# A decoder step on one core: 1,768 products of constants, lying in all 92 activation slots, ahead of the first conditioning product

## The chip, the cores and the metric

The kernel runs on one core of one Trainium2 chip. The metric is the device time of one execution in microseconds (us). Engines are called by the profile's names: PE is TensorE's matmul, PEld its weight load, DVE is VectorE, ACT is ScalarE, POOL is GpSimd, and SP issues the transfers.

## The reference, cut to what matters

One layer for 288 tokens (256 of a prompt, 8 times 4 of samples) with 2048 features:

```
mod = (silu(c) @ w_ada + b_ada)                  # conditioning, 9 vectors
h = rms(x) * (1 + sc_m) + sh_m
proj = h @ w_in                                  # gates, conv, u, v
merged = sigmoid(ga) * (ya @ w_pa) + sigmoid(gb) * (yb @ w_pb)
x = x + gt_m * (merged @ w_out)
h2 = rms(x) * (1 + sc_f) + sh_f
gate, up = split(h2 @ w_ffn_in)
x = x + gt_f * ((silu(gate) * up) @ w_ffn_out)
y = rms(x) * g_final
```

All data are float32. The kernel computes all of this before and after the change.

## The kernel before, in words

Activations lie with features on the 128 partitions and the 288 tokens along the row, one tile of 128 features after the other. A product is taken with both factors split in a high and a low part of type fp32r: `triple` (L222) issues three matmuls, high times high (L224), high times low (L227), low times high (L229), so that of each weight tile's two parts the high one is loaded into the array twice in a row. The moving operand is an activation of 288 columns (298 in the first products, where 10 conditioning columns ride along). It lies in one of 92 equal "slots" of SBUF (`SLOTS`, `slot`, L112), handed out and taken back by a pool. Weights stream in as 1 MB blocks into seven buffers (`RAW`, tag `raw`). ACT makes the high parts of a block (L448) and DVE the low ones (L454, or L243 in the paced first part).

The order of PE's work is the order in which the code is written. It starts with fillers, `warm` (L568), which multiply a constant bf16 tile `wb` by itself into a bank called `idle` that nobody reads: 24 of them, while the first transfers land. Then come the first conditioning product (`Ada.run`, L388, units `a0`) with fillers in between, and `first_tile` (L690): DVE turns the conditioning sums (L402), scales (L676, L678), ACT makes the high part of the first activation tile (L677), and PE begins with the weights `w0` (L501). `second_tile` (L701) does the same with unit `a1` for the second activation tile, whose weights are `wK`. The square sums, the normalisation and the later conditioning units are woven into the blocks that follow.

SP issues the loads in a fixed order in the head: `a0` (two buffers), `w0`, piece 0 of `x`, `a1` (two buffers), piece 1 of `x`, `wK`, then `wA` and the other pieces of `x` in turns. A load into a `raw` buffer waits until the last reader of what lay there is done, and what stands behind it on SP waits too.

Of the kernel before, what the change touches and what calls it, by code (L numbers as in the profile page):

```python
# [8 lines left out]
F32 = mybir.dt.float32  # L9
F32R = mybir.dt.float32r  # L10
# [4 lines left out]
P = 128  # L15
D = 2048
T = 288
TP = 256
TU = T + 10
# [4 lines left out]
SLOTS = 92  # L24
RAW = 7
# [59 lines left out]
def decoder_kernel(tc, d):  # L85
    nc = tc.nc
    from contextlib import ExitStack

    with ExitStack() as es:
        def pool(name, bufs=1, **kw):  # L90
            return es.enter_context(tc.tile_pool(name=name, bufs=bufs, **kw))

        pc = pool("const")
        pw = pool("wstream")
        pslot = pool("slots", SLOTS)
        ptmp = pool("tmp", 5)
        pps = pool("psum", 4, space=bass.MemoryType.PSUM)
        with tc.manual_schedule(engines={nc.tensor.engine}):
            _body(tc, nc, d, pc, pw, pslot, ptmp, pps)


def _body(tc, nc, d, pc, pw, pslot, ptmp, pps):
    ids = [0]

    def nm(s):
        ids[0] += 1
        return f"{s}_{ids[0]}"

    def const(name, shape, dt=F32):
        return pc.tile(shape, dt, tag=name, name=name)  # L110

    def slot(dt=F32, shape=(P, T)):  # L112
        return pslot.tile(list(shape), dt, tag="s", name=nm("s"), padded_shape=[P, TU])
# [4 lines left out]
    def psmain():  # L118
        return pps.tile([P, 512], F32, tag="main", name=nm("pm"), bufs=4)
# [4 lines left out]
    V, A, G, PE, SY = nc.vector, nc.scalar, nc.gpsimd, nc.tensor, nc.sync  # L124
# [227 lines left out]
    class Step:  # L352
        defer = False
        raw = None
# [209 lines left out]
    wb = const("wb", [P, 288], BF16)  # L564
    G.memset(wb, 1.0)
    idle = psmain()
# [475 lines left out]
        tail.close()  # L1042


    rh1 = h1.__getitem__
    def at(main, plan):
        out, n = [], 0
        for s in main:
            out.append(s)
            if isinstance(s, Blk):  # L1050
                n += 1
                out += plan.pop(n, [])
        assert not plan
        return out
# [70 lines left out]
    n = len(steps)  # L1125
# [30 lines left out]
    for s in steps:  # L1156
# [11 lines left out]
        i = pos[id(s)]  # L1168
# [124 lines left out]
```

## Time and profile before

| | |
|---|---|
| median of 2 runs | 1624.98 us (1624.95 to 1625.01) |
| the profiled execution | 1625.02 us, of which the span from the first to the last instruction is 1623.2 |
| mean granted PE clock | 0.998 |
| matmul records on PE | 12,645, some 11,300 of them of the split products |
| DVE, ACT, POOL busy | 63%, 45%, 1% of the span |
| HBM read | 352.46 MB, 219 GB/s over the span |

The page gives the share of the span in which each engine is busy, and the chain of work that ended last. A matmul's record (its "mean ns") lasts longer than the distance to the next one's start, since matmuls are pipelined. What one costs is the distance between starts, and over a stretch without a gap that is the stretch divided by the number of matmuls in it.

### The profile page before, as it was taken

How to read it: one execution, taken by the hardware profiler on the slowest of the kernel's cores; microseconds unless marked ns; L12 is line 12 of the kernel's file. 1: busy time of each engine (PE TensorE's matmuls, PEld its weight loads, DVE VectorE, ACT ScalarE, POOL GpSimd, SP SyncE). 2: the span in 40 equal slices, each digit the busy share in tenths (PEclk: the TensorE clock that was granted, in tenths of full speed). 3: DMA queues.
4: the chain of work that ended last, by engine and by line, in shares of the span. 5: the costliest groups of instructions: out<-in, count | busy, mean ns of one | idle time of the engine just before them, and what ended most of it. 6: DMA issues, size and time to landing. Idle time of an engine off the chain costs nothing.

```text
span 1623.2 us, 31599 instructions
## 1 busy us (share of the span) xinstructions
PE 1613.2 (99%) x12645; PEld 1549.3 (95%) x12645; DVE 1015.8 (63%) x2196; ACT 736.2 (45%) x1358; POOL 21.8 (1%) x66
## 2 busy tenths in 40 slices
PE   9999999999999999999999999999999999999997
PEld 8998999999999999999999999999999999999997
DVE  6676788877755567667744555555555555555565
ACT  5533344643444334456633444444444444444454
POOL 0000000000000000011000000000000000000000
PEclk9999999999999999999999999999999999999999
DMA  9887866777877666654576556453464434645341
GB/s 376 324 318 286 313 238 212 273 284 289 298 292 309 261 260 228 241 178 158 185 307 263 207 180 209 156 173 110 164 229 157 168 121 161 225 157 172 110 161 59
DMA packets 59140, 357.60 MB, mean 220 GB/s; under 512 B 6736, under 2 KB 9840, under 8 KB 28272
## 3 DMA queue, kind: packets, MB, share of 16 engines
q1 hardware_dynamic: 58704, 355.45, 60.0%
q8 instruction: 99, 1.62, 0.4%
q14 instruction: 49, 0.40, 0.1%
q10 hardware_dynamic: 288, 0.13, 0.0%
HBM read 352.46 MB, written 3.09 MB: 219 GB/s over the span
## 4 chain that ended last, share of the span: by engine, by line
PE 98%; DMA 1%; DVE 0%; DVEq 0%; ACT 0%; issue 0%; ACTq 0%
PE pm L224 31%; PE pm L227 31%; PE pm L229 30%; PE ada L388 5%; DMA raw<-in_wK 1%; DMA raw<-in_w 0%; DVE st L1023 0%; DMA ct<-in_c 0%; PE px L227 0%; PE px L818 0%; PE px L224 0%; PE px L229 0%; PE px L859 0%; PE px L198 0%; PE px L860 0%; PE px L861 0%
## 5 line engine op out<-in xcount | busy, mean ns | idle before, releaser
L224 PE MATMUL pm<-s,hi 128*128 128x288 f32 (+1 forms) x3750 | 1108.9, 296 | 0.0
L227 PE MATMUL pm<-s,hi 128*128 128x288 f32 (+1 forms) x3750 | 1105.0, 295 | 0.0
L229 PE MATMUL pm<-s,lo 128*128 128x288 f32 (+1 forms) x3738 | 1101.3, 295 | 0.0
L448 ACT CAST hi<-raw 128x512 fp32r<-128x512 f32 (+1 forms) x963 | 587.4, 612 | 812.0 <-PE pm L227 776.7
L454 DVE TENSOR_TENSOR lo<-raw,hi 128x512 fp32r<-128x512 f32 (+1 forms) x849 | 577.2, 681 | 439.2 <-ACT hi L448 426.8
L224 PEld LDWEIGHTS pm<-s,hi 128*128 128x128 f32 x3750 | 705.1, 188 | 15.2 <-issue 13.3
L227 PEld LDWEIGHTS pm<-s,hi 128*128 128x128 f32 x3750 | 704.7, 188 | 0.0
L229 PEld LDWEIGHTS pm<-s,lo 128*128 128x128 f32 x3738 | 702.7, 188 | 0.0
L243 DVE TENSOR_TENSOR lo<-raw,hi 128x512 fp32r<-128x512 f32 x111 | 74.7, 676 | 29.6 <-ACT hi L448 28.9
L388 PE MATMUL ada<-raw,cs 128*32 128x512 f32 (+2 forms) x1152 | 88.3, 452 | 0.0
L388 PEld LDWEIGHTS ada<-raw,cs 128*32 128x32 f32 x1152 | 30.9, 110 | 44.7 <-issue 42.0
L766 DVE TENSOR_TENSOR s<-pm,s 128x288 f32<-128x288 f32 x72 | 32.9, 457 | 19.8 <-PE pm L229 19.8
L298 DVE TENSOR_TENSOR s<-t,s 128x288 fp32r<-128x288 f32 (+1 forms) x76 | 34.6, 459 | 6.4 <-ACT s L296 6.4
L296 ACT CAST s<-t 128x288 fp32r<-128x288 f32 (+1 forms) x76 | 32.5, 433 | 12.9 <-DVE t L798 12.4
L338 DVE SCALAR_TENSOR_TENSOR x<-pm,mod,x 128x256 f32<-128x256 f32 x79 | 37.5, 475 | 0.0
L944 DVE SCALAR_TENSOR_TENSOR t<-t,pm 128x288 f32<-128x288 f32 x42 | 19.1, 454 | 20.6 <-PE pm L229 20.6
L758 DVE TENSOR_TENSOR s<-pm,s 128x288 f32<-128x288 f32 x48 | 21.8, 454 | 10.4 <-PE pm L229 9.5
L337 DVE TENSOR_TENSOR t<-pm,mod 128x32 f32<-128x32 f32 x79 | 15.2, 192 | 18.5 <-PE pm L229 18.5
L743 DVE SCALAR_TENSOR_TENSOR s<-pm,s 128x256 f32<-128x256 f32 x48 | 23.1, 480 | 4.1 <-PE pm L229 4.1
L749 DVE TENSOR_TENSOR s<-s,rb 128x288 f32<-128x288 f32 x48 | 21.5, 449 | 0.0
L172 ACT ACTIVATE t<-x 128x288 f32<-128x288 f32 x29 | 12.9, 445 | 17.4 <-DVE x L341 17.4
L177 DVE TENSOR_TENSOR acc<-acc,t 128x288 f32<-128x288 f32 x33 | 15.0, 456 | 8.2 <-ACT t L172 8.2
(158 smaller groups left out, 479.7 us busy)
## 6 DMA issues: line engine op xcount, KB each, us to landing
raw<-in_fi SPq DMA_DIRECT2D x84, 1024.0 KB, 4.9
raw<-in_a SPq DMA_DIRECT2D x64, 1024.0 KB, 8.8
raw<-in_f SPq DMA_DIRECT2D x64, 704.0 KB, 4.0
raw<-in_wD SPq DMA_DIRECT2D x34, 1024.0 KB, 5.7
raw<-in_aE SPq DMA_DIRECT2D x16, 1024.0 KB, 10.3
raw<-in_wo SPq DMA_DIRECT2D x16, 1024.0 KB, 6.4
raw<-in_wC SPq DMA_DIRECT2D x19, 768.0 KB, 5.7
raw<-in_pa SPq DMA_DIRECT2D x8, 1024.0 KB, 5.9
```

The lines of the kernel that those rows point to most:

```text
L224: PE.matmul(out, wh, ah, start=first, stop=False)
L227: end_ = PE.matmul(out, wh, al, start=False, stop=turn and last)
L229: end_ = PE.matmul(out, wl, ah, start=False, stop=last)
L243: lows.pop(0)[1]()
L296: A.copy(hi, a)
L298: V.tensor_tensor(lo, a, hi.bitcast(F32), ALU.subtract)
L338: V.scalar_tensor_tensor(x[:, m, :TP], ps[:, :TP], mod[:, gt0 + m, 0:1], x[:, m, :TP], ALU.mult, ALU.add)
L388: PE.matmul(acc[32 * j : 32 * j + 32, :w], cs[:, kt, :], self.raw[:, o : o + w], start=kt == 0, stop=kt == 15, tile_position=(0, 32 * j), ...
L448: A.copy(hi, self.raw[:, s * 128 : e * 128])
L454: sub()
L743: V.scalar_tensor_tensor(t[:, :TP], ps[:, :TP], t[:, T : T + 1], t[:, :TP], ALU.add, ALU.add)
L766: V.tensor_tensor(a, ps[:, :T], a, ALU.add)
```

## The change

A function `bench` is written behind `finish` and called before anything of the steps is issued. It takes three of the seven `raw` buffers (`f`, `r0`, `r1`) and all 92 slots, fills them with the constant 0.75 (DVE and ACT in turns) and lets PE multiply them. `r0` gives the weights, the first 128 columns of it (`w`) in all but the last group. Each product goes to the bank `idle` with 288 columns, and none is read.

```
+    def bench():
+        f = pw.tile([P, 2048], F32, tag="raw", name=nm("bench"), bufs=RAW)
+        V.memset(f, 0.75)
+        rs = []
+        for i in range(2):
+            r = pw.tile([P, 2048], F32R, tag="raw", name=nm("benchr"), bufs=RAW)
+            A.copy(r, f) if i else V.tensor_copy(r, f)
+            rs.append(r)
+        r0, r1 = rs
+        ms = []
+        for i in range(SLOTS):
+            m = slot(F32R, (P, TU))
+            (A.copy if i % 2 else V.tensor_copy)(m, f[:, :TU])
+            ms.append(m)
+
+        def mm(s, m):
+            PE.matmul(idle[:, :T], s, m, start=True, stop=True)
+
+        w = r0[:, :P]
+        for i in range(48):
+            mm(wb[:, :P], wb)
+        for o in range(0, 64, 4):
+            for i in range(12):
+                mm(w, r1[:, o : o + T])
+        for o in range(0, 512, 64):
+            for i in range(8):
+                mm(w, r1[:, o : o + T])
+        for n in range(1, SLOTS):
+            for i in range(4):
+                mm(w, ms[0][:, :T])
+                mm(w, ms[n][:, :T])
+        for n in range(0, 22):
+            for i in range(4):
+                mm(w, ms[0][:, 8 : 8 + T])
+                mm(w, ms[n][:, 8 : 8 + T])
+        for n in range(0, 22):
+            for i in range(4):
+                mm(w, ms[0][:, :T])
+                mm(w, ms[n][:, 8 : 8 + T])
+        for step, o in ((1, 0), (2, 0), (3, 0), (4, 0), (5, 0), (1, 8), (4, 8), (1, 4)):
+            for i in range(16):
+                k = i % 8
+                ah, al = (ms[(2 * k + j) * step][:, o : o + T] for j in (0, 1))
+                mm(r0[:, P * k : P * k + P], ah)
+                mm(r0[:, P * k : P * k + P], al)
+                mm(r0[:, 1024 + P * k : 1024 + P * k + P], ah)
+
+    bench()
```

On PE (lines are those of the changed kernel, where `bench`'s matmuls all have line 1061) the end of the 48 bf16 products, the 256 of one tile of constants, and the first pairs of slots stand before everything else; the names are `wb` (the bf16 constant), `benchr` (`r0` is 99, `r1` is 101) and `s` (a slot):

```order
L1061 LDWEIGHTS wb
L1061 MATMUL pm_96<-wb 128x288
L1061 MATMUL pm_96<-benchr_101,benchr_99 128x288 x256
L1061 MATMUL pm_96<-s_103,benchr_99 128x288
L1061 MATMUL pm_96<-s_105,benchr_99 128x288
```

The fillers of line 571 and the conditioning products, which were PE's first rows, now come behind all of these.

On DVE the copies into slots stand ahead of the turning of the first conditioning sums (L402):

```order
L153 MEMSET cs 128x512
L1047 MEMSET bench_97 128x2048
L1051 CAST benchr_99<-bench_97 128x2048
L156 SCALAR_TENSOR_TENSOR ctt<-ctt,ct 128x144
L1057 CAST s_103<-bench_97 128x298
L157 TENSOR_SCALAR cs<-ctt 128x16x9
L692 TENSOR_SCALAR bada_93<-cp_74 128x2
L1057 CAST s_107<-bench_97 128x298
```

Another 44 such copies follow before L402, which before stood directly behind L692. On ACT 46 copies into slots and the one into `r1` likewise stand ahead of the first high part of a weight block (L448). SP's rows keep their order; but its eighth to tenth `raw` buffers (the second of `a1`, `wK`, the first `wA`) are now those of `f`, `r0` and `r1`.

## The prediction

> **What bounds the kernel now.** I read the page first, for which engine sets the end:
>
> ```profile
> span 1623.2 us, 31599 instructions
> PE 1613.2 (99%) x12645; PEld 1549.3 (95%) x12645; DVE 1015.8 (63%) x2196; ACT 736.2 (45%) x1358; POOL 21.8 (1%) x66
> PE 98%; DMA 1%; DVE 0%; DVEq 0%; ACT 0%; issue 0%; ACTq 0%
> L224 PE MATMUL pm<-s,hi 128*128 128x288 f32 (+1 forms) x3750 | 1108.9, 296 | 0.0
> L227 PE MATMUL pm<-s,hi 128*128 128x288 f32 (+1 forms) x3750 | 1105.0, 295 | 0.0
> L224 PEld LDWEIGHTS pm<-s,hi 128*128 128x128 f32 x3750 | 705.1, 188 | 15.2 <-issue 13.3
> L227 PEld LDWEIGHTS pm<-s,hi 128*128 128x128 f32 x3750 | 704.7, 188 | 0.0
> ```
>
> PE holds 98% of the chain that ended last and waits for almost nothing; PE work put ahead of everything else is therefore paid in full, unless the start has idle time to hide it. A record's 295 ns is not a matmul's price, since records overlap. For the price I took a long stretch of PE alone that holds only products of 288 columns (view by stretches: length, busy time with count, granted clock, share of the transfer engines, GB/s), and two short ones out of it:
>
> ```profile
> 1000.00:1600.00 600.00, 600.00 (x4540) 1.00 0.47 158
> 1180.00:1200.00 20.00, 20.00 (x154) 1.00 0.75 245
> 1580.00:1600.00 20.00, 20.00 (x154) 1.00 0.00 1
> ```
>
> Two of the 4540 began before the stretch, so 600/4538 = **132.2 ns** per fp32r product of 288 columns. The short stretches hold the same 154 with the transfer engines at 75% and at rest: the price is PE's own, and the quiet that the added products will find around them does not cheapen it. L227 repeats the weights of L224 and still has a load of its own of 188 ns for each.
>
> Third, the start, in order of time:
>
> ```profile
> 1.07 0.48 DVE L153 MEMSET cs<- 128x512 f32 x1
> 1.12 5.24 PE L571 MATMUL pm<-wb 128*128 128x288 bf16 x24 [1.12 <-POOL wb L565]
> 4.83 0.32 ACT L155 ACTIVATE ctt<-ct 128x144 f32<-128x144 f32 x1 [1.90 <-DMA ct<-in_c]
> 6.29 1.10 PE L388 MATMUL ada<-raw,cs 128*32 128x64 f32 x64
> 10.05 1.15 PE L571 MATMUL pm<-wb 128*128 128x288 bf16 x8
> 10.19 0.25 DVE L402 STREAM_TRANSPOSE ev<-ada 128x64 f32<-128x64 f32 x1 [3.64 <-PE ada L388]
> 11.36 0.82 PE L501 MATMUL pm<-s,hi 128*128 128x298 f32 x4 [0.15 <-ACT s L677]
> ```
>
> Useful work begins at 6.29 us, after 24 fillers, and the first product of the weights (L501) at 11.36. From the first conditioning product to L501 are 5.07 us, a chain of PE, DVE (L402) and ACT.
>
> **The change part by part.** Nothing is removed. In `bench` PE gets 48 bf16 products of the kind of L571, then 16x12 + 8x8 = 256 of one tile, 91x8 = 728 of pairs, 22x8 + 22x8 = 352 of shifted pairs, 8x16x3 = 384 of triples: 1,720 fp32r products of 288 columns.
>
> *The 48 bf16 products.* They need only `wb`, so they start at 1.12 as the fillers did. The row at 1.12 gives the time of 24, the eight at 10.05 the warm distance, and the tile's row the length of one record, which is to be taken off both:
>
> ```profile
> L571 PE MATMUL pm<-wb x54: 282/286/448, 1.1 to 1614.1; 128*128 128x288 bf16 x54
> ```
>
> The 24th starts 5.24 - 0.29 = 4.95 us after the first, over slow distances to begin with (a record of 448 ns against 286 shows it). Warm, a distance is (1.15 - 0.29)/7 = 0.123 us. From the 24th it is 25 warm distances to the first fp32r product, which starts at 1.12 + 4.95 + 25 x 0.123 = **9.15 us**.
>
> *The constants must be there by then.* No such memset, copy or size is in the trace; the nearest rows are L153 (512 columns in 0.48 us) and these:
>
> ```profile
> L584 ACT ACTIVATE q<-x 128x1152 f32<-128x1152 f32 x3 | 3.5, 1175 | 0.0
> L587 DVE TENSOR_TENSOR q<-q,q 128x1152 f32<-128x1152 f32 x2 | 2.7, 1349 | 0.0
> L737 DVE COPY s<-pm 128x298 f32<-128x298 f32 x19 | 8.6, 464 | 4.4 <-PE pm L229 3.3 <-PE pm L227 1.0 <-PE pm L509 0.2
> L296 ACT CAST s<-t 128x298 fp32r<-128x298 f32 x16 | 6.9, 432 | 0.0
> ```
>
> DVE: `f` in 4 x 0.48 = 1.9 us behind L153, done at 3.5; `r0` in 1.349 x 2048/1152 = 2.4, done at 5.9. ACT: `r1` behind L155, from 5.15 for 1.175 x 2048/1152 = 2.1, done at 7.3. Both lie ahead of 9.15, so I cost them at nothing; the cover is the 48 bf16 products, and without them PE would wait 7.3 - 1.1 = 6.2 us. The 92 slots take 46 x 0.464 = 21.3 us on DVE and 46 x 0.432 = 19.9 on ACT, both done near 28 us. PE asks for the second slot only after 256 products, at 9.15 + 256 x 0.1322 = 43.0: cost nothing, by 15 us. A copy of twice the price would cost nothing either.
>
> *The 1,720 products.* No row shows a constant weight tile against changing slots, nor one moving tile repeated, nor slots shifted by 8 columns. From below I bound them by the bf16 products of the same 288 columns (0.123), from above by fp32r products with 10 columns more:
>
> ```profile
> 25.80 0.30 PE L227 MATMUL pm<-s,hi 128*128 128x298 f32 x1
> 26.62 0.30 PE L227 MATMUL pm<-s,hi 128*128 128x298 f32 x1
> ```
>
> These two are six distances apart, 0.82/6 = 0.137. The sum is 211.6 us from below, 235.6 from above, and 1720 x 132.2 ns = **227.4** by the row of the same type and width, which I take: 4,538 products over many slots lie behind it, and it holds repeated weights (L227) as well as changing ones.
>
> The Trainium skill (TensorE: Matmul & The Clock Gate, Back-to-back issue gap) gives a warm matmul's gap as N/2.4 + 2.5 ns, which is 122.5 for 288 columns. The bf16 fillers agree (123 ns); the fp32r products of this kernel, at 132.2, do not. By the Trainium skill's formula the 1,720 would take 210.7 us.
>
> *What follows the products.* They end at 9.15 + 227.4 = 236.5. The program then goes on with its 24 fillers, now all warm: 24 x 0.123 = 2.95, and the first conditioning product starts at 239.5. Before, these fillers hid the wait for `ct` and `a0`; now they hide nothing and are paid. `ct` and the blocks of `a0`, `w0` and the first of `a1` have buffers from the start and landed long before. With the same 5.07 us, L501 comes at 244.6 instead of 11.36: a shift of **233.2 us**.
>
> *Transfers.* The second block of `a1` takes the buffer of `f`, free near 28 us; piece 1 of `x` is queued on SP behind it. Both have 200 us to land. `wK` takes the buffer of `r0`, free only with the last product at 236.5, and behind it on SP stand all `wA` blocks, three quarters of `x` and the rest. What that costs is read from how late `wK` was before:
>
> ```profile
> 10.53 9.19 DMA raw<-in_wK
> 19.79 0.52 ACT hi L448
> 21.01 0.34 PE L226 MATMUL px<-s,lo 128*128 128x298 f32 x1
> 21.69 0.40 PE L227 MATMUL px<-s,hi 128*128 128x298 f32 x1 [0.34 <-DVE s L687]
> ```
>
> (The first two are of the chain that ended last.) `wK` landed at 19.72, its high part followed at once and held up DVE's making of the second tile; L227 came 0.68 us after L226 instead of 0.137, so 0.5 us were lost. After the change `wK` is asked for at 236.5, and if it takes 9.2 us again it is there at 245.7; 19.72 moved by 233.2 is 252.9. It and all behind it come 7 us earlier against PE than before, so the cost is nothing and the gain **0.5 us**. If the queue started later than I think, by over 7 us, PE would wait for it microsecond for microsecond.
>
> *Where the main part's slots lie.* `bench` takes and returns every slot once, and of the 12,030 products of the built program behind it only 102 keep the address of their moving operand. Whether the address matters, no row tells by itself; the two stretches of 20 us above have the same count, so not by much on the mean over many slots. I take nothing, and allow 0.3 ns on 11,300 products, 3.4 us either way.
>
> *Sum.* 1623.2 + 233.2 - 0.5 = 1855.9 us of span. The profiled execution took 1625.02, 1.82 more than its span, and stands 0.04 over the median: 1855.9 + 1.8 = **1857.7 us**. Its own range is 1851 to 1864: 2 ns on the 1,720 (3.4 us) and 3.4 for the slots.
>
> **The rivals.**
>
> *A: the added products run at the bf16 distance,* because the weights stay the same or nothing else is read. For it: in 1,336 of the 1,720 the weights never change. Against: L227's unchanged weights are loaded anew, 188 ns as L224's, and a stretch without transfers is no faster. Price 1720 x (132.2 - 123) = 15.8 us less: 1841.9. By the Trainium skill's formula (same page and section) it would be 16.7 less.
>
> *B: constants at fixed addresses collide,* the common first slot with the others or the weights with the slots, and each product costs what 298 columns cost. For it: `ms[0]` and `w` come back in over a thousand products, so a bad pair isn't averaged away. Against: the main products run through fixed pairs of slots too, block after block, and no stretch shows it. Price 1720 x (137 - 132.2) = 8.3 us more: 1866.
>
> *C: not slower. The products are dropped on the way to the chip,* since nobody reads `idle`. Then the slot copies decide: they stand ahead of L402 on DVE, which then comes near 28 us instead of 10.19, and the time is 1625 + 17.8 = 1643, 1.1% more and within 2%. It decides from some 1,520 vanished products on, (233.2 - 32.5)/0.132. Against it: the fillers of L571 are never read either and all 54 stand in the trace.
>
> **How the numbers follow.** A measurement of this kernel tells about 2% (32.5 us) from no change. The forecast has 0.84, A 0.06, B 0.08, C 0.02. The time is the forecast's, 1857.7. The range reaches from 1850 to 1866: the forecast's own with a microsecond more below, and above up to B; A and C, 0.08 together, stay out. Forecast, A and B are all slower by over 2%: 0.98; C is within 2%: 0.02; no case is faster.
>
> **What would show it.** In the changed profile: 1,768 more matmuls, line 1061; the first fp32r one near 9.15 us and the first of the slots near 43; the stretch 50:230 with a count that gives 132 ns; L388 first near 239.5 and L501 near 244.6; DVE and ACT idle from 28 us to 239; no wait of 0.34 us at the second tile; and from L501 on a remainder of 1611 us, 1623.2 - 11.36 less the stall. A count of 1/0.123 per us would mean A, 1/0.137 B. I am wrong in the main step if the products take another price, wrong in the transfers if PE waits for `wK`, and wrong about the slots if the remainder behind L501 changes by more than 3 us.

## The result, and the profile after

The changed kernel takes 1860.86 us (median of 2 runs, 1860.51 to 1861.2) against 1624.98: a ratio of 1.145 (1.140 to 1.150), 235.9 us more. The forecast was 1857.7.

From the page of the kernel after the change, the span, the engines, the chain, and one new group:

```profile
span 1859.0 us, 35237 instructions
PE 1849.2 (99%) x14413; PEld 1783.9 (96%) x14413; DVE 1029.6 (55%) x2244; ACT 753.5 (41%) x1405; POOL 21.3 (1%) x66
PE 99%; DVE 0%; DVEq 0%; issue 0%; ACT 0%; POOL 0%; POOLq 0%
L1061 PE MATMUL pm<-s,benchr 128*128 128x288 f32 x1464 | 194.3, 295 | 0.0
```

PE has 1,768 records more and is busy for 236 us more, in a span longer by 236. The views in order of time show where the terms came out (start, duration, engine, line):

```profile
1.12 8.73 PE L1061 MATMUL pm<-wb 128*128 128x288 bf16 x48 [1.12 <-POOL wb L565]
9.60 2.63 PE L1061 MATMUL pm<-benchr,benchr 128*128 128x288 f32 x18
...
237.66 3.11 PE L571 MATMUL pm<-wb 128*128 128x288 bf16 x24
240.71 1.10 PE L388 MATMUL ada<-raw,cs 128*32 128x64 f32 x64
245.92 0.82 PE L501 MATMUL pm<-s,hi 128*128 128x298 f32 x4 [0.29 <-ACT s L677]
```

The fp32r products run from 9.60 to 237.66, so one costs 228.06/1720 = 132.6 ns. Then follow the fillers, 3.05 us that hide nothing, and the chain of 5.2 us to L501.

The view by stretches, of PE alone, has the pairs of slots (44 to 139), the shifted pairs (140 to 163, 164 to 186), the triples (187 to 237), and the main part's stretch that answers to 1000 to 1600 of before:

```profile
44.00:139.00 95.00, 95.00 (x719) 1.00 0.02 5
140.00:163.00 23.00, 23.00 (x175) 1.00 0.00 1
164.00:186.00 22.00, 22.00 (x168) 1.00 0.01 1
187.00:237.00 50.00, 50.00 (x379) 1.00 0.00 1
1236.00:1836.00 600.00, 600.00 (x4540) 1.00 0.46 157
```

Less the two under way at each beginning, these are 132.5, 132.9, 132.5 and 132.6 ns, and 132.2 in the main part: constants, unchanged weights and pairs of any kind cost what the real products cost, to half a per cent.

The filling was done long before it was needed, in the group of the copies (duration min/median/max, first and last start):

```profile
L1057 DVE CAST s<-bench x46: 302/306/310, 5.3 to 16.2; 128x298 fp32r<-128x298 f32 x46
L1057 ACT CAST s<-bench x46: 434/439/443, 6.8 to 22.2; 128x298 fp32r<-128x298 f32 x46
```

On SP, and at the second activation tile:

```profile
43.73 0.33 SPq L432 DMA_DIRECT2D raw<-in_wK  x1
237.85 0.33 SPq L432 DMA_DIRECT2D raw<-in_wA  x1
...
255.38 0.30 PE L226 MATMUL px<-s,lo 128*128 128x298 f32 x1
255.72 0.19 PEld L227 LDWEIGHTS px<-s,hi 128*128 128x128 f32 x1 [0.28 <-DVE s L687]
255.72 0.40 PE L227 MATMUL px<-s,hi 128*128 128x298 f32 x1
```

`wK` was asked for at 43.73, not at 236.5: it took the buffer of `r1`, whose last reader is the 256th fp32r product, and `wA` that of `r0`. At the second tile 0.34 us lie between the two products instead of 0.68. PE still waits there for DVE (L687), though `wK` has long landed.

One thing is not in these lines. From L501 to the end the span was 1623.2 - 11.36 = 1611.9 us before, and is 1859.0 - 245.9 = 1613.1 now, though 0.3 us less are lost at the second tile. The experiments are mostly about this.

### The profile page after: what moved, and what is told of

Same layout as the page of the kernel before. It is cut to its first block, busy times and chain, and to the rows that moved or that the text cites. A ratio compares the mean times of both kernels' runs of the same rounds, so it can differ in the third digit from the quotient of the medians.

```text
span 1859.0 us, 35237 instructions
## 1 busy us (share of the span) xinstructions
PE 1849.2 (99%) x14413; PEld 1783.9 (96%) x14413; DVE 1029.6 (55%) x2244; ACT 753.5 (41%) x1405; POOL 21.3 (1%) x66
## 4 chain that ended last, share of the span: by engine, by line
PE 99%; DVE 0%; DVEq 0%; issue 0%; ACT 0%; POOL 0%; POOLq 0%
PE pm L224 27%; PE pm L227 27%; PE pm L229 27%; PE pm L1061 13%; PE ada L388 5%; PE pm L571 0%; DVE st L1023 0%; PE px L227 0%; PE px L224 0%; PE px L818 0%; PE px L229 0%; PE px L859 0%; PE px L860 0%; PE px L198 0%; PE px L861 0%; PE px L995 0%
## 5 line engine op out<-in xcount | busy, mean ns | idle before, releaser
L448 ACT CAST hi<-raw 128x512 fp32r<-128x512 f32 (+1 forms) x963 | 587.3, 612 | 806.8 <-PE pm L227 773.5
L1061 PE MATMUL pm<-s,benchr 128*128 128x288 f32 x1464 | 194.3, 295 | 0.0
L1061 PEld LDWEIGHTS pm<-s,benchr 128*128 128x128 f32 x1464 | 194.2, 188 | 0.0
L402 DVE STREAM_TRANSPOSE ev<-ada 128x512 f32<-128x512 f32 (+2 forms) x9 | 4.8, 534 | 238.3 <-PE ada L388 238.3
L766 DVE TENSOR_TENSOR s<-pm,s 128x288 f32<-128x288 f32 x72 | 32.8, 455 | 20.8 <-PE pm L229 20.7
L1061 PE MATMUL pm<-benchr,benchr 128*128 128x288 f32 x256 | 34.1, 295 | 0.0
L1061 PEld LDWEIGHTS pm<-benchr,benchr 128*128 128x128 f32 x256 | 33.9, 188 | 0.0
```

The lines of the kernel that those rows point to most:

```text
L448: A.copy(hi, self.raw[:, s * 128 : e * 128])
L766: V.tensor_tensor(a, ps[:, :T], a, ALU.add)
L1061: PE.matmul(idle[:, :T], s, m, start=True, stop=True)
```

## Experiments

All kernels compute the whole reference. "Behind L501" is the span from the first L501 to the last instruction, from the trace. The runs "once", "in bf16", "by width and type" and "the filling alone" were executed once each; the others from two to ten times. Theory T: the time is the count of products times their price, and all of it is paid. Theory S: the part behind L501 changed because its slots lie at other addresses.

**The same products without slots.** In place of the loops over `ms`:

```
-        for n in range(1, SLOTS):
...
+        for i in range(1464):
+            mm(w, r1[:, :T])
```

> Same 48 + 1,720 products as the change, but all 1,720 read one tile (r1) and no slot is taken, so the main part has its old slot addresses back. Theory S (the part behind the first weight product L501 is 1.2 us longer after the change than before only because its slots lie elsewhere; without that it would be 0.5 us shorter): span behind L501 1611.3 us, as before less the stall at the second tile; with 1,720 x 131.7 ns ahead of it about 1857.5 us in all. Rival (it is longer because raw buffers or late loads moved): span behind L501 stays near 1613.1, in all about 1859.3.

Measured: 1854.86 us (1854.82 to 1855.3), 1609.5 behind L501. The rival is out: `bench` still takes its three `raw` buffers here, and nothing is longer. The direction is that of theory S, the size is not: it is 1.8 us below what S expected. In the built program 98% of the split products (11,112 of 11,328) have their old slot addresses, but not all. Counted from L501, and by the times of the kernel before, the same products of the two traces run apart by 0.7 us in the first 27 us, where no address differs (0.34 of it is the second tile, the rest is not explained). They run apart by 1.1 between 85 and 293 us and by 0.5 behind 606 us, in stretches where some addresses differ (115 of 1,399 products and 72 of 7,349). From 293 to 606 us none of 2,051 addresses differs, and they keep their distance to the ns.

**Every pair and triple once.** In all loops the repeats are cut, for instance:

```
-            for i in range(4):
+            for i in range(1):
```

> Every pair and triple of the change once instead of 4, 8, 12 or 16 times: 486 fp32r products, and four fifths of the main part's slot addresses as after the change. Theory (count times 132.6 ns, all of it paid): 1,234 products less are 163.6 us less, L501 at 82.3 us, in all 1697; span behind L501 near 1613 as after the change, by theory S. Rival (part of the added time is not per product): L501 later than 84. Rival to S (the length of the head counts): span behind L501 near 1611.5.

Measured: 1696.33 us, L501 at 81.1, 1613.1 behind it. (The triples ran twice in the change, not 16 times.) Theory T holds over 1,234 products fewer (164.8 us at L501, 163.6 expected). The part behind L501, with 83% of the split products at the change's addresses, does not care how long the head is.

**The same count in bf16.**

```
-            PE.matmul(idle[:, :T], s, m, start=True, stop=True)
+            PE.matmul(idle[:, :T], wb[:, :P], wb, start=True, stop=True)
```

> Slots and tiles are filled as in the change, but all 1,768 products are bf16 products of the filler tile with 288 columns. Theory (the price is that of the type): 1,720 x 122.5 ns = 210.7 instead of 228.1, L501 near 228.5, in all 1842 to 1845 (the slots of the main part lie in a third order). Rival (constants of one tile cost what they cost, whatever the type): 1860.

Measured: 1843.98 us, L501 at 228.4. Its stretch by the same view:

```profile
20.00:215.00 195.00, 195.00 (x1594) 1.00 0.04 12
```

This is 122.5 ns. Rival A's price is that of bf16; constants in fp32r don't get it.

**Without the fillers behind `bench`.**

```
-    steps = [Do(lambda: warm(24)), a0[0], Do(lambda: warm(5)), a0[1]]
+    steps = [a0[0], Do(lambda: warm(5)), a0[1]]
```

> The change without the 24 fillers behind it, all addresses as after the change. Theory (behind the products the fillers hide nothing): 24 x 0.1225 = 2.9 us less, 1857.9; span behind L501 1613.1 to a tenth. Rival (something else is not ready at once, the first conditioning product or the first high part): less than 1 us gained.

Measured: 1857.59 us (1857.29 to 1857.79), 3.3 less, and 1613.1 behind L501. Three us are the fillers; the rest is a start of the products 0.4 earlier. Fillers are free only where there is something to wait for.

**The price by width and type.** In place of the loops:

```
+        for n in (64, 128, 192, 256, 288, 320, 384, 448, 512):
+            for i in range(64):
+                mm(w, r1[:, :n])
...
+                mm(h0[:, :P], h1_[:, :n])
+        for c in (96, 64, 32):
+            for i in range(64):
+                mm(w[:, :c], r1[:, :T])
```

> Behind the 48 fillers, 64 products each of nine widths from 64 to 512 columns in fp32r (weights and moving tile constant), the same nine widths in bf16 (the same bytes read as bf16), and 64 each of 288 fp32r columns against weights of 96, 64 and 32 columns. Theory P (fp32r columns stream slower): price proportional to the columns, 0.459 ns each, 235 ns at 512 and 118 at 256, and no change with narrower weights. Rival F (a fixed 12 ns per product on top of the bf16 rate, from loading the weights): 225 ns at 512, 119 at 256, and 123 ns at 288 with 32 columns of weights. bf16: 122.5 at 288, 216 at 512.

Measured, as the mean distance of the starts of each group's third to 63rd product (ns):

```
columns     64    128    192    256    288    320    384    448    512
fp32r      111*   213*   112*  120.0  131.7  146.7  173.4  206.7  227.2
bf16      29.2   55.8   82.5  109.2  122.5  135.8  162.5  189.2  216.3
288 fp32r columns, weights of 96, 64, 32 columns: 133.3, 130.1, 131.2
```

(* not this mean, since 64 and 192 columns ran in part, and 128 wholly, at half the clock, see the last section: 111 and 112 are the distances at the full clock, 213 that at half.) Six of the stretches, fp32r with 256, 288 and 512 columns, then bf16 with 256 and 288, and 288 against weights of 32 columns:

```profile
45.00:51.00 6.00, 6.00 (x52) 1.00 0.00 0
52.00:59.00 7.00, 7.00 (x55) 1.00 0.01 2
95.00:107.00 12.00, 12.00 (x55) 1.00 0.00 1
119.00:125.00 6.00, 6.00 (x57) 1.00 0.01 3
127.00:133.00 6.00, 6.00 (x51) 1.00 0.00 0
196.00:203.00 7.00, 7.00 (x56) 1.00 0.01 2
```

Rival F has the shape right and its cause wrong: fp32r costs 9 to 11 ns more than bf16 at five of the six widths from 256 on (11 at both 256 and 512), so it is nearly a fixed amount and not a share; 448 columns, with 17.5 ns, fall out of line. But narrower weights don't take it away. What it comes from stays open. The Trainium skill (TensorE: Matmul & The Clock Gate, Back-to-back issue gap) gives the gap as N/2.4 + 2.5 ns; all nine bf16 widths agree to 0.5 ns (216.3 against 215.8 at 512), fp32r does not.

**The filling alone.** The 1,768 products are replaced by

```
+        for m in ms:
+            mm(w, m[:, :T])
```

> The slots and the two tiles are filled as in the change, but instead of its 1,768 products PE reads every slot once (92 products). Theory (the filling is hidden only by the products ahead of it): DVE is done at 16.5 us and ACT at 22.6 as after the change, PE waits for them, then come the fillers (3 to 5 us, partly at a slow clock) and the chain of 5.1: L501 at 31 to 33 instead of 11.4, in all 1645 to 1648. Rival (the filling costs nothing by itself): 1637, 92 products of 132 ns more.

Measured: 1648.08 us. On PE, in order of time:

```profile
5.72 0.61 PE L1061 MATMUL pm<-s,benchr 128*128 128x288 f32 x1 [5.72 <-DVE s L1057]
7.28 15.80 PE L1061 MATMUL pm<-s,benchr 128*128 128x288 f32 x91 [0.95 <-ACT s L1057]
22.93 3.11 PE L571 MATMUL pm<-wb 128*128 128x288 bf16 x24
```

PE is kept until 22.9 by copies and not by its 92 products (12 us). Without its cover the filling costs 19.7 us (L501 at 31.1); 2.9 us more come behind L501, where the slots lie in a fourth order; that the order is the reason is not shown by this run.

**Addresses alone, nothing added.** Into the kernel before, ahead of the first step:

```
+    for _ in range(45):
+        m = slot(F32R, (P, TU))
+        G.memset(m[:, :1].bitcast(F32), 0.0)
```

> The kernel before, with 45 slots taken, touched by a one-column memset on POOL and given back ahead of the first step: no product added, nearly all slots of the main part at other addresses. Theory S: L501 stays at 11.4 us, the span behind it changes by between 0.3 and 2.5 us, either way. Rival (addresses don't matter, the 1.2 us came from the added work): it stays at 1611.9 to 0.1.

Measured: 1629.24 us, ratio 1.0026 (1.0016 to 1.0035); L501 at 11.1 and 1616.5 behind it, 4.6 us more. That is beyond the 2.5 that I gave theory S. But for the 45 small memsets on POOL nothing else was added, and the loss grows all along the main part (0.3 us by 270 us behind L501, 2.3 by 570, 3.1 by 990), with PE as busy as before. From 1000 to 1580:

```profile
1000.00:1580.00 580.00, 580.00 (x4377) 1.00 0.48 163
```

Less two under way that is 132.6 ns a product; the kernel before has 132.2 there.

> As the run before with 23 slots taken and given back, which leaves two fifths of the main products' addresses as they were. Theory S: a change behind L501 of another size, between 0.2 and 2 us either way, and none in the stretches where the addresses are the same. Rival: 1611.9 to 0.1.

Measured: 1627.06 us, ratio 1.0012 (1.0002 to 1.0022), L501 at 12.1 and 1613.4 behind it, 1.6 us more. The second half of what was expected can't be read here: products with old and new addresses alternate, and no long stretch has the old ones alone. The run without slots has such a stretch. Theory S stands: the order in which slots are handed out moves the main part by some microseconds, with no wait to be seen anywhere.

**All slots at one place in 256 bytes.** The change's own products show one thing that matters about an address. The pairs' price, as the mean of the eight distances of a pair, runs through 133.2, 131.9, 132.5, 132.4 ns with the slot number, and again every four slots; four slots of 1216 bytes are 19 times 256. For one tile repeated (`r1`, 12 products at each of 16 offsets), the mean of the fourth to the eleventh distance from start to start, by the bytes from the weights' place in 256 to the activations':

```
bytes    0     16     32     48     64     80     96    112
ns   131.6  131.6  133.3  132.5  131.9  131.0  131.6  135.1
bytes  128    144    160    176    192    208    224    240
ns   133.3  130.1  133.0  130.9  133.4  133.8  133.3  131.3
```

In the kernel before all weights lie at 96 of 256 and the slots in nearly equal shares at 32, 96, 160 and 224. So I made slots of 1280 bytes, 88 for room, and shifted their data. The second form, at 240, is as follows; the first has `OFF = 0` and no `gap`, the third a `gap` of 24 columns in place of 32.

```
-SLOTS = 92
+SLOTS = 88
+OFF = 4
...
+        pool("gap").tile([P, 32], F32, tag="gap", name="gap")
...
-        return pslot.tile(list(shape), dt, tag="s", name=nm("s"), padded_shape=[P, TU])
+        p, n = shape
+        return pslot.tile([p, n + OFF], dt, tag="s", name=nm("s"), padded_shape=[P, 320])[:, OFF:]
...
-    ones = const("ones", [P, P])
+    ones = const("ones", [P, 64])
```

> The kernel before, with nothing added: a slot is 1280 bytes instead of 1216, so that all begin at the same place in 256 bytes (96, as the weights do), 88 slots instead of 92 for room, the unread part of a constant tile cut. Theory Q (a product's price follows from where its moving operand begins in 256 bytes against its weights; one tile repeated there cost 131.6 ns after the change, the main part's mixed places 132.2): 11,300 x 0.6 = 6 us less, 1619. Rival (a loop over one weight tile tells nothing of products whose weights change): 1622 to 1628. Four slots less could add a wait of PE, to be seen as idle time.

> As the run before, with every slot's data beginning 144 bytes further in 256 (240). The tile repeated at that place cost 130.1 ns. Theory Q: 11,300 x 2.1 = 23 us less than before, 1602. Rival: 1622 to 1628, as the first.

> As the run before, at 208 bytes of 256, where the repeated tile cost the most, 135.1 ns. Theory Q: 11,300 x 2.9 = 33 us more than before, 1658. Rival: 1622 to 1628, as the other two.

Measured: 1620.09 us at 96 (ratio 0.997, 0.9958 to 0.9981), **1603.82** at 240 (0.9871, 0.9856 to 0.9885), 1640.11 at 208 (1.0093, 1.0073 to 1.0113). The stretch from 1000 to 1580 of the kernel before, then of these three:

```profile
1000.00:1580.00 580.00, 580.00 (x4389) 1.00 0.48 163
```
```profile
1000.00:1580.00 580.00, 580.00 (x4407) 1.00 0.48 162
```
```profile
1000.00:1580.00 580.00, 580.00 (x4464) 1.00 0.47 160
```
```profile
1000.00:1580.00 580.00, 580.00 (x4352) 1.00 0.48 162
```

Less two under way these are 132.2, 131.7, 130.0 and 133.3 ns. Theory Q is right in the order and in two of three sizes; at 208 the main part, whose weights change, loses 1.1 ns in this stretch and not 2.9. The loop over one weight tile is thus a guide and not a measure. The 5 us won at 96 are no more than the order of slots alone moved above, so that form proves little by itself; the 21 and 15 us of the other two are well beyond it. The four slots less add no wait of PE over 0.3 us.

**Weights and slots moved together.** To the form at 240:

```
+    pw.tile([P, 16], F32, tag="gap2", name="gap2", bufs=1)
```

> As the run with all slots at 240, with the high and low weight tiles and the slots both moved on by 64 bytes: weights at 160 of 256 instead of 96, slots at 48 instead of 240. Theory R (what counts is the distance from the weights' place to the activations', 144 bytes): no change, 1603 to 1605. Rival A (the activations' place alone counts; at 48 the repeated tile cost 133.8 ns against 130.1 at 240): about 1636 to 1645.

Measured: 1604.19 us (ratio 0.9872, 0.9856 to 0.9889). With activations at 48, the rival's bad place, but still 144 bytes from the weights, nothing is lost:

```profile
1000.00:1580.00 580.00, 580.00 (x4463) 1.00 0.47 160
```

So, as far as one move of 64 bytes tells, it is the distance between the two operands' places that counts when all products have the same one.

This does not explain theory S. In the kernel before, a product of 288 columns that another follows at once costs on the mean 131.5, 132.1, 132.8 and 132.3 ns at distances of 0, 64, 128 and 192 bytes. With 45 slots turned over the shares of the four hardly change, and at these prices the new shares add 0.1 us and not 4.6. Of its 11,328 split products 8,106 even keep their distance, and it is these that cost 0.55 ns more each, 4.4 us together. In the change the new shares account for 0.7 us of some 1.5. What else in the addresses, or in their order, moves the main part stays open.

## Why the prediction was right, and where it was off

Against its span of 1855.9 the measured one is 1859.0, 3.1 us more:

| step of the prediction | said | measured |
|---|---|---|
| 48 bf16 products, first fp32r at | 9.15 | 9.60 |
| 1,720 fp32r products | 227.4 | 228.1 |
| fillers and chain to L501 | 8.0 | 8.3 |
| from L501 to the end | 1611.3 | 1613.1 |

*That PE sets the end and added PE work is paid in full*: right. L501 comes 234.6 us later of the 235.9 in all, and with just over a quarter of the count (486 products) it holds as well.

*The price of 132.2 ns from the row of the same type and width*: right to 0.4 ns. Between its two ends, 123 and 137, neither rival came near: A's price needs bf16 (1844), and a bad distance as in B does exist (135.1 at 112 bytes), but only 12 of the 1,720 products have it, and the returning first slot costs no more than other slots (131.9 to 133.2 in its pairs).

*The 48 products*: 0.45 us too early. I took the number of slow ones from the kernel before; the trace has 22 distances of 240 ns now and 17 then. The granted clock rises from half to full at 6.6 us now and at 5.5 then, and at other times again in other runs (4.9 us with 45 slots moved, 5.6 without the fillers).

*The constants at no cost*: right; DVE was done at 16.5 and ACT at 22.6 instead of 28, and the products ahead, which I named as the cover, are worth 19.7 us, as the filling alone shows.

*Transfers*: the named buffer was wrong and harmless. I numbered the buffers in the order of the calls; the pool gave `wK` the one that came free first, that of `r1`. The gain at the second tile was 0.34 us, not 0.5: part of that wait was DVE's own work for the tile (L687), which I had put down to the late `wK` alone.

*Where the main part's slots lie, taken as nothing*: this step was mis-sized, and is the largest miss, 1.8 us, of which 0.2 is the smaller gain at the second tile. The allowance of 3.4 either way held it, but that was luck: nothing in the reasoning bounds it at that. The reason given for it, that two stretches show the same count, was too weak: each averages over many slots. With no product added, 45 slots turned over cost 4.6 us, more than was allowed.

*Rival C*: in all kernels the products that nobody reads are there.

## What to carry to other kernels

On a kernel that PE bounds, an added product costs the distance of starts in a gapless stretch of the same type and width, to about 1% whatever is in it; look for its cover only at the start, and count again what the cover used to hide. When nothing waits and the time still moves by a few tenths of a per cent, compare the addresses of the two programs. Here choosing the distance between weights and activations in 256 bytes was worth 1.3% (1603.8 against 1625.0), more than all the time in which PE stood idle (10 us).

## What the runs showed of the hardware that I had not expected

The price of an fp32r product of 288 columns runs from 130.0 to 133.3 ns in the same kernel with the distance between its operands' places in 256 bytes, where all products have one distance. It repeats: over 313 us, with the slots the same, executions of two programs keep their distance to the ns.

In fp32r a product of 64 columns costs as much as one of 192: 111 and 112 ns at the full clock, 213 at half. One of 128 costs 213 at half too; at the full clock it was not measured. The half clock was the second surprise. In the run by widths PE has a product under way all the time, and yet:

```profile
10.00:20.00 10.00, 10.00 (x61) 0.63 0.69 266
24.00:39.00 15.00, 15.00 (x72) 0.50 0.00 0
40.00:50.00 10.00, 10.00 (x88) 1.00 0.00 0
```

The granted clock fell to 0.50 at 12.6 us, 3.4 us after the 64-column products began at 9.2, stayed there through those of 128, and came back at 39.9, in the group of 192 columns. So what brings it down is not idle time as the profile counts it. It may be how little of the time columns stream. From the bf16 widths a column takes 0.418 ns at the full clock, (216.3 - 29.2)/448, so 64 columns stream for 27 of 111 ns. At half the clock a column takes 240/288 = 0.833 ns, so those of 128 stream for 107 of 213 ns and those of 192, where the clock came back, for 160. That reading is an inference from one run. The bf16 products of 64 columns, each starting 29 ns after the last, did not bring the clock down, but they lasted 1.9 us, less than the 3.4 above, and decide nothing. The Trainium skill (TensorE: Matmul & The Clock Gate, Part 1) has a gate with two rates, half and full, set by how busy PE has been; the rates agree with this run (0.50 and 1.00). What the run adds is that a PE without a gap in the profile can still fall to the lower one.
